# Hybrid attention and short-convolution step: full-height score matmuls, gating units moved last, attention tiles re-placed

## The chip, the cores and the metric

One core of one Trainium2 chip runs the whole kernel. The metric is device time in microseconds (us) of one launch; lower is better. Each engine has its own in-order stream of instructions: TensorE (PE) does matmuls, VectorE (DVE) and ScalarE (ACT) read and write SBUF and PSUM, GpSimd (POOL) does elementwise work, and SyncE (SP) here does little but issue DMAs, in the order in which they were written into its stream.

## The reference, cut to what matters

```python
x = x + 0.5 * rmsnorm(swiglu(rmsnorm(x, f1_pre), f1_wg, f1_wu, f1_wd), f1_post)      # FFN 1
proj = rmsnorm(x, m_pre) @ w_in          # q | k | v | gate B | gate C | conv input
o = attend(q, k, v, lam)                 # 4 heads, two softmax maps per head, width 64 each
u = gate_c * hc
y = sum(conv_w[j] * u_ext[:, j:j + t] for j in range(3))     # u_ext: 2 state rows ahead of u
c_out = gate_b * y
x = x + rmsnorm(concat([o, c_out]) @ w_out, m_post)
x = x + 0.5 * rmsnorm(swiglu(rmsnorm(x, f2_pre), f2_wg, f2_wu, f2_wd), f2_post)      # FFN 2

def diff_attend(q, k, v, q_pos, k_pos, lam):
    s = einsum('bqhcd,bkhcd->bhcqk', q, k) * HEAD_DIM ** -0.5       # c: the two maps
    p = softmax(where(k_pos <= q_pos, s, NEG_INF))
    return einsum('bhqk,bkhe->bqhe', p[:, :, 0] - lam * p[:, :, 1], v)
```

There are 1040 prompt tokens (16 of them meta tokens) and 8 sample sequences of 8 tokens each, which also attend to 1024 past positions held in pages of 128. All data are float32.

## The kernel before

**Precision.** TensorE reads operands in a reduced 32-bit format (fp32r in the rows). To keep float32 results each operand is split by `halves` into a high half (a copy by ACT, L168) and a low half (the original minus the high half, by DVE, L169, or POOL), and a product is made of three matmuls: high x high, high x low, low x high.

**Stages.** FFN 1, then the mixer's projections, then attention, then the output projection, then FFN 2. The 1104 tokens are held in two halves (p = 0 and 1, in the SBUF tiles X0 and X1 with row scales R), features on partitions.

**Projections.** `seven` runs a list of jobs (u, p): unit u of the weights (256 columns of `w_in`, two of the 128-wide column groups paired by `PAIRS`) for token half p. A job is seven products in Strassen's manner, 84 matmuls of 128x276, evicted by ACT and DVE in steps (L347, L350, L353, L356 and the `c..` functions of the unit). The raw weights of one unit lie in one buffer WR (a 1 MB DMA `WR<-in_w_in`); `weights_piece` adds blocks of WR in place on DVE (L273, L275, L277, L279) and writes the seven pieces of the one weight set W (L168, L169). The next unit's load into WR is issued when the last piece of the current one has been made. Units 0 to 5 are q, k and v (`Unit2`). `Product` units multiply gate C and the conv input into `cu` and, with token half 1, call `conv_ready`: three-tap convolution on DVE into `cy`, and DMAs of the new conv state, `out_conv_p` and `out_conv_s`, the latter 1024 rows of 8 bytes. `Gated` units multiply gate B with `cy` into `co` and store that to DRAM (`c_spill`). In the order before, unit 8 is gated and uses the convolutions of 6 and 7; unit 11 is gated and uses those of 9 and 10.

**Attention.** After the projections SP issues the constants `cst`, the queries and keys of head 0 (`load_qk`: one DMA of 128x1040 each), values, lambdas, and the pages of keys and values (`kp`, `vp`; each needs an index read from the page table). `prompt_jobs` makes scores, softmax, transposes (`fl`, L818), and value products (`po`, L833) of one head, block of 128 queries by block; `sample` stages (`sa`, L875, L910) are interleaved with it. In `scores` a head's two maps lie in partitions 0 to 63 and 64 to 127 of the same tile, so a score matmul uses 64 rows of the array (`tile_position`), and the six matmuls of a piece of keys (three passes, two maps) are issued map by turns. PE, DVE, ACT and SP each run their streams in the order in which a scheduler put the instructions.

Of the kernel before, what the change touches and what calls it, by code (L numbers as in the profile page):

```python
# [9 lines left out]
F32R = mybir.dt.float32r  # L10
I32 = mybir.dt.int32
AF = mybir.ActivationFunctionType
ALU = mybir.AluOpType
# [22 lines left out]
         (16, 20), (17, 21), (12, 13), (18, 22), (19, 23), (14, 15)]  # L36
# [7 lines left out]
def hybrid_step(ctx: ExitStack, tc: tile.TileContext, ins, outs, n_pool):  # L44
# [11 lines left out]
    def nm(s):  # L56
        uid[0] += 1
        return f"{s}_{uid[0]}"
# [90 lines left out]
    def dma(dst, src):  # L149
        got = sync.dma_start(dst, src)  # L150
        last_dma[0] = got.ins
        return got
# [13 lines left out]
    def halves(hi, lo, raw, on):  # L166

        act.activation(hi, raw, AF.Copy)  # L168
        on.tensor_tensor(lo, raw, f32(hi), op=ALU.subtract)  # L169
# [337 lines left out]
    def first_jobs(n):  # L507

        return [(0, 0), (1, 0), (1, 1), (0, 1)] + [(u, p) for u in range(2, n) for p in range(2)]
# [82 lines left out]
    cy = [Y[0][:, 1106 + 1104 * n:][:, :1104] for n in range(2)]  # L592
# [4 lines left out]
    def conv_ready(j):  # L597

        taps = [misc[:, j * 3 + t:j * 3 + t + 1] for t in range(3)]
        y, us = cy[j % 2], cs[j % 2]  # L600
# [38 lines left out]
    class Gated(Parts):  # L639


        def __init__(self, j, p):
            self.j, self.p = j, p
            self.o = [co[2 * p], co[2 * p + 1]]

        def put(self, n, g, t):
            y = cy[n][:, self.p * HT + g * G:][:, :G]
            gp.tensor_tensor(self.o[n][:, g * G:g * G + G], t, y, op=ALU.mult)
# [10 lines left out]
        def c21(self, ps):  # L659
            dve.scalar_tensor_tensor(self.o[1][:, :G], ps, -1.0, cy[1][:, self.p * HT:][:, :G], op0=ALU.mult, op1=ALU.mult)  # L660
            for n in range(2):
                dma(c_spill[self.j + n][:, self.p * HT:self.p * HT + HT], self.o[n])

    def mixer_unit(u, p):
        if u < 6:
            return Unit2(u, p)
        return Gated(2 * (u // 9), p) if u in (8, 11) else Product({6: 0, 7: 1, 9: 2, 10: 3}[u], p)

    seven(first_jobs(12), lambda u: ins["w_in"][u], mixer_unit, background)


# [6 lines left out]
    def ring(name, n, w, dt=F32):  # L678
        return [mix.tile([P, w], dt, tag=f"{name}{x}", name=nm(name)) for x in range(n)]


    kpages, vpages = ring("kp", 8, 512), ring("vp", 8, 512)
# [4 lines left out]
    qs_t, = ring("qs", 1, 1024)  # L687
    qs = qs_t.rearrange("p (h b q) -> p h b q", h=H, b=DB)
    ks = ring("ks", 1, 320)[0].rearrange("p (h k) -> p h k", h=H)
# [3 lines left out]
    Q = [ring(f"q{n}", 4, TP, F32R) for n in range(2)]  # L693
    pbuf = ring("p", 6, TP)
    abuf = [a.rearrange("p (j q) -> p j q", j=9) for a in ring("at", 4, 1152)]
    vbuf = [v.rearrange("p (j e) -> p j e", j=9) for v in ring("vs", 2, 1152)]
    tq = ring("t", 10, 256)
    cst, = ring("cst", 1, K_W)
    onesV, = ring("onesV", 1, P)
# [8 lines left out]
    dma(cst, ins["consts"])  # L708

    def load_qk(h):  # L710
        ql, kl, qh, kh = Q[h % 2]
        for lo, hi, src in ((ql, qh, q_spill[h]), (kl, kh, k_spill[h])):
            dma(f32(lo), src[:, :TP])
            halves(hi, lo, f32(lo), dve)
# [5 lines left out]
    load_qk(0)  # L720
    load_v(0)
# [37 lines left out]
    def prompt_jobs(h):  # L759

        pairs = {}
        ql, kl, qh, kh = Q[h % 2]
        vt_ = vbuf[h % 2]

        def scores(qi):
# [7 lines left out]
            for x in range(npc):  # L773
# [3 lines left out]
                for n, (a, b) in enumerate(((qh, kh), (qh, kl), (ql, kh))):  # L777
                    for m in range(2):
                        r = slice(m * DH, (m + 1) * DH)
                        last_pe[0] = nc.tensor.matmul(pw[m], a[r, q0:q0 + P], b[r, k0:k1], start=n == 0, stop=n == 2,  # L780
                                                      tile_position=(m * DH, 0)).ins
# [294 lines left out]
```

## Time and profile before

| | |
|---|---|
| median of 3 runs | 2342.27 us (2340.71 to 2344.84) |
| profiled execution, its own time | 2346.7 us |
| its span | 2344.9 us |
| mean granted TensorE clock | 0.945 of full speed |

The span is the time from the first to the last profiled instruction; what lies around it is 1.8 us. A granted clock of 1.00 in a row is TensorE's upper level (2.4 GHz), 0.50 its lower (1.2 GHz); values in between are means over a stretch with both.

### The profile page before, as it was taken

The page shows a single profiled execution, that of the slowest core. Times are in us where ns is not written, and L with a number is a line of the kernel's source. Part 1 is how long each engine was busy: PE and PEld are TensorE (multiplying, and loading weights), DVE is VectorE, ACT ScalarE, POOL GpSimd, SP SyncE. Part 2 cuts the span into 40 slices and gives each one's busy share as a digit, 9 for nine tenths or more (in the row PEclk, how much of TensorE's full clock was granted, in tenths as well). Part 3 has the DMA queues.
Part 4 walks back from the last instruction along what each step waited for, and adds up shares of the span by engine and source line. Part 5 has one row for each costly group of instructions (what it writes and reads, how often), then busy time and mean ns, then how long its engine had stood idle before and what let it go on. Part 6 is the DMA issues. An engine that isn't in the chain of part 4 may idle for free.

```text
span 2344.9 us, 40781 instructions
## 1 busy us (share of the span) xinstructions
PE 2123.6 (91%) x16266; PEld 2036.9 (87%) x16266; DVE 1373.3 (59%) x2698; ACT 908.3 (39%) x1830; POOL 325.5 (14%) x360
## 2 busy tenths in 40 slices
PE   4899999999999759989689989749999999999995
PEld 4899999999999659989567659749999999999995
DVE  7866666662343985455357653777666666713436
ACT  8533333343211553322245444465333333522112
POOL 0111111121110002221201111001111111301100
PEclk9999999999999879999779979879999999999997
DMA  6122222242332223422557424212122212522213
GB/s 214 56 84 79 75 70 84 79 167 74 110 100 67 96 79 130 141 48 56 174 189 236 162 85 143 78 62 79 63 82 79 84 61 84 174 83 91 98 48 116
DMA packets 106112, 239.29 MB, mean 102 GB/s; under 512 B 20898, under 2 KB 36706, under 8 KB 98274
## 3 DMA queue, kind: packets, MB, share of 16 engines
q1 hardware_dynamic: 105922, 236.70, 30.1%
q8 instruction: 127, 2.08, 0.4%
q14 instruction: 63, 0.52, 0.1%
HBM read 182.35 MB, written 58.82 MB: 103 GB/s over the span
## 4 chain that ended last, share of the span: by engine, by line
PE 78%; DVE 11%; DMA 5%; ACT 3%; issue 2%; SPq 1%; POOL 0%; DVEq 0%; ACTq 0%
PE mm L162 23%; PE mm L163 23%; PE mm L164 23%; DVE X L169 2%; PE qk L780 2%; PE po L833 2%; DMA WR<-in_w_in 2%; DVE W L169 1%; DVE Y L469 1%; PE fl L818 1%; PE sa L910 1%; PE sa L875 1%; DVE ss L210 1%; DVE Y L467 1%; DMA WR<-in_w_gu 1%
## 5 line engine op out<-in xcount | busy, mean ns | idle before, releaser
L162 PE MATMUL mm<-X,W 128*128 128x276 f32 x4224 | 1240.8, 294 | 141.1 <-ACT X L168 100.6
L163 PE MATMUL mm<-X,W 128*128 128x276 f32 x4224 | 1238.7, 293 | 13.4 <-DVE X L169 12.8
L164 PE MATMUL mm<-X,W 128*128 128x276 f32 x4224 | 1234.2, 292 | 5.2 <-DVE W L169 5.2
L162 PEld LDWEIGHTS mm<-X,W 128*128 128x128 f32 x4224 | 803.6, 190 | 148.5 <-ACT X L168 104.2
L163 PEld LDWEIGHTS mm<-X,W 128*128 128x128 f32 x4224 | 804.3, 190 | 17.9 <-DVE X L169 16.3
L164 PEld LDWEIGHTS mm<-X,W 128*128 128x128 f32 x4224 | 805.0, 191 | 7.2 <-DVE W L169 6.7
L168 ACT ACTIVATE W<-WR 128x512 fp32r<-128x512 f32 (+1 forms) x437 | 292.7, 674 | 614.5 <-PE mm L163 526.4
L169 DVE TENSOR_TENSOR W<-WR,W 128x512 fp32r<-128x512 f32 (+1 forms) x437 | 333.9, 766 | 194.0 <-ACT W L168 164.4
L367 POOL TENSOR_TENSOR n<-n,R 128x276 f32<-128x276 f32 x88 | 70.2, 798 | 675.1 <-ACT n L378 675.1
L449 DVE TENSOR_TENSOR Y<-Y,mm 128x276 f32<-128x276 f32 x128 | 56.2, 440 | 168.2 <-PE mm L164 168.0
L350 DVE TENSOR_TENSOR n<-mm,n 128x276 f32<-128x276 f32 x112 | 49.8, 445 | 155.2 <-PE mm L164 155.1
L347 ACT ACTIVATE n<-mm 128x276 f32<-128x276 f32 x224 | 87.7, 392 | 117.0 <-PE mm L164 105.0
L367 POOL TENSOR_TENSOR u<-u,R 128x276 f32<-128x276 f32 x88 | 77.9, 885 | 292.2 <-ACT u L378 292.2
L169 POOL TENSOR_TENSOR X<-X 128x552 fp32r<-128x552 f32 x46 | 75.8, 1658 | 303.0 <-ACT X L168 275.7
L169 DVE TENSOR_TENSOR X<-X 128x552 fp32r<-128x552 f32 x58 | 65.2, 1147 | 79.5 <-ACT X L168 79.5
L163 PE MATMUL mm<-X,X 128*128 128x276 f32 x288 | 83.8, 291 | 2.6 <-DVE X L169 2.6
L168 ACT ACTIVATE X<-X 128x552 fp32r<-128x552 f32 x104 | 66.3, 660 | 48.0 <-DMA X<-hid 41.5
L163 PE MATMUL mm<-X 128*128 128x276 f32 x288 | 84.2, 292 | 0.0
L209 ACT ACTIVATE sq<-Y 128x552 f32<-128x552 f32 x84 | 55.5, 661 | 73.8 <-DVE Y L488 36.3
L780 PE MATMUL qk<-q,q 64*128 64x400 f32 (+10 forms) x360 | 69.5, 392 | 16.1 <-ACT q L168 13.9
L162 PE MATMUL mm<-X,X 128*128 128x276 f32 x288 | 83.5, 290 | 0.0
L164 PE MATMUL mm<-X,X 128*128 128x276 f32 x288 | 83.4, 290 | 0.0
(152 smaller groups left out, 2428.4 us busy)
## 6 DMA issues: line engine op xcount, KB each, us to landing
WR<-in_w_gu SPq DMA_DIRECT2D x46, 1024.0 KB, 5.1
hid<-Y SPq DMA_DIRECT2D x88, 276.0 KB, 2.1
X<-hid SPq DMA_DIRECT2D x88, 276.0 KB, 4.0
WR<-in_w_dnm SPq DMA_DIRECT2D x24, 768.0 KB, 4.2
kp<-in_cache_k SPq DMA_DIRECT2D x64, 256.0 KB, 4.3
vp<-in_cache_v SPq DMA_DIRECT2D x64, 256.0 KB, 4.3
WR<-in_w_in SPq DMA_DIRECT2D x13, 1024.0 KB, 5.4
Y<-in_x SPq DMA_DIRECT2D x16, 276.0 KB, 5.8
```

Of the source, the lines that this page charges most:

```text
L162: nc.tensor.matmul(ps, lh, rh, start=first, stop=False, **kw)
L163: nc.tensor.matmul(ps, lh, rl, start=False, stop=False, **kw)
L164: last_pe[0] = nc.tensor.matmul(ps, ll, rh, start=False, stop=last, **kw).ins
L168: act.activation(hi, raw, AF.Copy)
L169: on.tensor_tensor(lo, raw, f32(hi), op=ALU.subtract)
L209: act.activation(sq, src, AF.Square)
L347: act.activation(t, ps, AF.Copy)
L350: dve.tensor_tensor(self.n1, ps, self.n1, op=ALU.add)
L367: on.tensor_tensor(t, t, lay["R"][p][:, g * G:g * G + G], op=ALU.mult)
L449: dve.tensor_tensor(y, y, ps, op=ALU.add)
L780: last_pe[0] = nc.tensor.matmul(pw[m], a[r, q0:q0 + P], b[r, k0:k1], start=n == 0, stop=n == 2, tile_position=(m * DH, 0)).ins
L833: nc.tensor.matmul(po[:, off:off + rows], vt_[:kr, j, :], at[:kr, j, :rows], start=j == 0, stop=j == qi)
```

## The change

There are three parts. First, `PAIRS` and the job list: units 6 to 9 become the four `Product` units, units 10 and 11 the two `Gated` ones, and the last four jobs are (10,0), (11,0), (11,1), (10,1), so that token half 0 is finished two jobs before the end; unit 10's weights are loaded twice. The four convolution results get four places (`cy`). Second, `load_qk` and `scores`: for each head and map there is a tile q0 or q1 with the high half of 64 query features in partitions 0 to 63 and the low half in 64 to 127, and key tiles kh and kl with the same high or low half in both; a score is two full-height matmuls, q x kh and q x kl, instead of three half-height ones. Each source is loaded twice, into both partition halves. Third, the tiles of the attention stage are allocated in another order, so that the queries and keys of head 0, `cst`, `qs`, `ks`, the small tiles `t` and the pages `kp` take the place of X0, and the queries of head 0 are loaded ahead of `cst`.

```diff
 PAIRS = [(0, 1), (4, 5), (2, 3), (6, 7), (8, 9), (10, 11),
-         (16, 20), (17, 21), (12, 13), (18, 22), (19, 23), (14, 15)]
+         (16, 20), (17, 21), (18, 22), (19, 23), (12, 13), (14, 15)]
...
-    cy = [Y[0][:, 1106 + 1104 * n:][:, :1104] for n in range(2)]
+    cy = [Y[0][:, 1106:2210], Y[0][:, 2210:3314], Y[1][:, 1104:2208], Y[1][:, 0:1104]]
...
-        return Gated(2 * (u // 9), p) if u in (8, 11) else Product({6: 0, 7: 1, 9: 2, 10: 3}[u], p)
-
-    seven(first_jobs(12), lambda u: ins["w_in"][u], mixer_unit, background)
+        return Gated(2 * (u - 10), p) if u >= 10 else Product(u - 6, p)
+
+
+    seven(first_jobs(10) + [(10, 0), (11, 0), (11, 1), (10, 1)], lambda u: ins["w_in"][u], mixer_unit, background)
...
+    scores_of = lambda x: {n: mix.tile([P, TP], F32R, tag=f"{n}{x}", name=nm(n)) for n in ("q0", "q1", "kh0", "kl0", "kh1", "kl1")}
+    cst, = ring("cst", 1, K_W)
+    Q = [scores_of(0)]
...
+    tq = ring("t", 10, 256)
+    kpages = ring("kp", 8, 512)
...
-    dma(cst, ins["consts"])
-
     def load_qk(h):
-        ql, kl, qh, kh = Q[h % 2]
-        for lo, hi, src in ((ql, qh, q_spill[h]), (kl, kh, k_spill[h])):
-            dma(f32(lo), src[:, :TP])
-            halves(hi, lo, f32(lo), dve)
+
+        t = Q[h % 2]
+        for m in range(2):
+            q, kh, kl = t[f"q{m}"], t[f"kh{m}"], t[f"kl{m}"]
+            r = slice(m * DH, m * DH + DH)
+            for i in range(2):
+                at = slice(i * DH, i * DH + DH)
+                dma(f32(q[at]), q_spill[h][r, :TP])
+                dma(f32(kl[at]), k_spill[h][r, :TP])
+            act.activation(kh[DH:], f32(q[DH:]), AF.Copy)
+            dve.tensor_tensor(q[DH:], f32(q[DH:]), f32(kh[DH:]), op=ALU.subtract)
+            act.activation(q[:DH], f32(q[:DH]), AF.Copy)
+            halves(kh, kl, f32(kl), dve)
...
     load_qk(0)
+    dma(cst, ins["consts"])
     load_v(0)
...
-                for n, (a, b) in enumerate(((qh, kh), (qh, kl), (ql, kh))):
-                    for m in range(2):
-                        r = slice(m * DH, (m + 1) * DH)
-                        last_pe[0] = nc.tensor.matmul(pw[m], a[r, q0:q0 + P], b[r, k0:k1], start=n == 0, stop=n == 2,
-                                                      tile_position=(m * DH, 0)).ins
+                for m in range(2):
+                    for n in range(2):
+                        last_pe[0] = nc.tensor.matmul(pw[m], t[f"q{m}"][:, q0:q0 + P], t[f"{('kh', 'kl')[n]}{m}"][:, k0:k1],
+                                                      start=n == 0, stop=n == 1).ins
```

**SP, the second half of the projections.** Here SP's stream before, from the state DMAs of the first convolution to those of the fourth (Y_79 and Y_80 are the tiles Y[0] and Y[1]):

```order
L150 DMA out_conv_p<-Y_79 128x2
L150 DMA out_conv_s<-Y_79 1024x1x2
L150 DMA WR<-in_w_in 128x2048
...
L150 DMA c_spill_161<-Y_80 128x552
L150 DMA WR<-in_w_in 128x2048
L150 DMA out_conv_p<-Y_79 128x2
L150 DMA out_conv_s<-Y_79 1024x1x2
L150 DMA WR<-in_w_in 128x2048
L150 DMA WR<-in_w_out 128x1024 x2
L150 DMA out_conv_p<-Y_79 128x2
L150 DMA out_conv_s<-Y_79 1024x1x2
L150 DMA c_spill_162<-Y_80 128x552
```

And of the change, the same stretch from the third convolution on:

```order
L150 DMA out_conv_p<-Y_79 128x2
L150 DMA out_conv_s<-Y_79 1024x1x2
L150 DMA WR<-in_w_in 128x2048
L150 DMA out_conv_p<-Y_79 128x2
L150 DMA out_conv_s<-Y_79 1024x1x2
L150 DMA WR<-in_w_in 128x2048
L150 DMA c_spill_160<-Y_80 128x552
L150 DMA c_spill_161<-Y_80 128x552
L150 DMA WR<-in_w_in 128x2048
L150 DMA c_spill_162<-Y_80 128x552
```

Before, three of the four state DMAs had a load of `w_in` right behind them and the fourth none; now all four have one, and a further load (unit 10 again) stands behind the first `c_spill` pair.

**SP, from the last projection to the first scores.** Before:

```order
L150 DMA c_spill_162<-Y_80 128x552
L150 DMA WR<-in_w_out 128x1024
L150 DMA c_spill_163<-Y_80 128x552
L150 DMA cst_11242<-in_consts 128x1090
L150 DMA q_673_11212<-q_spill_147 128x1040
L150 DMA q_674_11213<-k_spill_151 128x1040
L150 DMA vs_11230<-v_spill 128x1024
L150 DMA vs_11230<-v_spill 16x128
L150 DMA t_11232<-in_lams 128x256
```

Now:

```order
L150 DMA c_spill_161<-Y_80 128x552
L150 DMA q_650_11208<-q_spill_147 64x1040
L150 DMA kl_653_11211<-k_spill_151 64x1040
L150 DMA q_650_11208<-q_spill_147 64x1040
L150 DMA kl_653_11211<-k_spill_151 64x1040
L150 DMA q_651_11209<-q_spill_147 64x1040
L150 DMA kl_655_11213<-k_spill_151 64x1040
L150 DMA q_651_11209<-q_spill_147 64x1040
L150 DMA kl_655_11213<-k_spill_151 64x1040
L150 DMA cst_11207<-in_consts 128x1090
L150 DMA vs_11235<-v_spill 128x1024
L150 DMA t_11216<-in_lams 128x256
```

The loads of head 0 stand behind the last `c_spill` in both, ahead of `cst` now, and there are eight of them instead of two.

**PE, scores of one query block of head 0.** Before (behind the arrow the key tile, then the query tile; 675 and 676 are the high halves, 673 and 674 the low ones):

```order
L780 MATMUL qk_11879<-q_676_11215,q_675_11214 128x320
L780 MATMUL qk_11879<-q_674_11213,q_675_11214 128x320
L780 MATMUL qk_11879<-q_676_11215,q_673_11212 128x320
L875 MATMUL sa_11657<-kp_11193,qs_11208 32x128 x4
L875 MATMUL sa_11657<-kp_11190,qs_11208 32x128 x4
L780 MATMUL qk_11880<-q_676_11215,q_675_11214 128x320
L875 MATMUL sa_11657<-kp_11194,qs_11208 32x128 x4
...
L780 MATMUL qk_11880<-q_674_11213,q_675_11214 128x320
L780 MATMUL qk_11880<-q_676_11215,q_673_11212 128x320
L780 MATMUL qk_11889<-q_676_11215,q_675_11214 128x336
L780 MATMUL qk_11890<-q_676_11215,q_675_11214 128x336
```

Now:

```order
L794 MATMUL qk_11955<-kh_652_11210,q_650_11208 128x384
L794 MATMUL qk_11955<-kl_653_11211,q_650_11208 128x384
L889 MATMUL sa_11684<-kp_11231,qs_11214 32x128 x4
L889 MATMUL sa_11684<-kp_11228,qs_11214 32x128 x4
L794 MATMUL qk_11956<-kh_654_11212,q_651_11209 128x384
L794 MATMUL qk_11956<-kl_655_11213,q_651_11209 128x384
```

A piece (one pair of qk numbers) had six rows, some of them with the two maps in turn and some with one map's three in a row; it has four now, always one map after the other.

## Rows read from the trace of the kernel before

**Rows 1.** By stretch: us; busy (count) of PE, PEld, DVE, ACT, POOL; PEclk, DMA, GB/s.
```profile
1163.00:1183.00 20.00, 8.46 (x98) 5.71 (x97) 4.37 (x22) 1.33 (x4) 3.44 (x17) 0.50 0.56 174
1202.00:1348.00 146.00, 142.06 (x1305) 98.74 (x1304) 98.77 (x370) 74.14 (x194) 18.20 (x24) 1.00 0.59 192
1348.00:1372.00 24.00, 23.73 (x80) 15.68 (x81) 12.61 (x54) 9.77 (x27) 3.03 (x4) 0.50 0.30 94
```

**Rows 2.** Waits of PE, 880 to 1180: total us, times, longest.
```profile
PE qk L780 <- ACT q L168: 13.9, 1, 13.9
PE mm L162 <- DVE n L353: 12.1, 3, 4.3
PE sa L875 <- POOL qs L746: 7.5, 4, 6.8
```

**Rows 3.** Chain that ended last, 1009 to 1028: start, us, what.
```profile
1010.37 0.13 PE mm L162
...
1013.44 10.47 DMA WR<-in_w_in
...
1025.04 0.60 PE mm L162
1025.64 0.23 PE mm L163
```

**Rows 4.** By stretch, behind the first and the last of three stalls (columns of rows 1).
```profile
1025.04:1032.00 6.96, 6.96 (x35) 6.96 (x36) 4.09 (x7) 0.92 (x2) 1.93 (x2) 0.59 0.00 0
...
1102.32:1108.00 5.68, 5.68 (x32) 5.68 (x33) 3.73 (x7) 0.88 (x2) 1.94 (x2) 0.70 0.00 0
```

**Rows 5.** SP's issues, 1136 to 1164: start, us, what.
```profile
1138.06 0.42 SPq L150 DMA_DIRECT2D c_spill<-Y  x1
1142.73 0.33 SPq L150 DMA_DIRECT2D cst<-in_consts  x1
...
1145.03 0.43 SPq L150 DMA_DIRECT2D t<-in_lams  x1
...
1163.63 0.43 SPq L150 DMA_DIRECT2D t<-q_spill  x1
```

**Rows 6.** Tile q, 1130 to 1400: min/median/max ns, first and last start, forms.
```profile
L168 ACT ACTIVATE q<-q x8: 1055/1070/1072, 1147.8 to 1281.5; 128x1040 fp32r<-128x1040 f32 x8
L169 DVE TENSOR_TENSOR q<-q,q x8: 1236/1242/1244, 1148.9 to 1283.5; 128x1040 fp32r<-128x1040 f32 x8
...
DMA to landing us min/median/max: 4.5/6.3/7.3
```

**Rows 7.** L780 alone, by stretch: us, busy (count) of PE and PEld, PEclk.
```profile
1202.00:1348.00 146.00, 40.17 (x248) 26.13 (x246) 1.00 0.59 192
1348.00:1372.00 24.00, 11.93 (x42) 8.18 (x42) 0.50 0.30 94
```

**Rows 8.** PE's timeline, 1299 to 1312: start, us, what.
```profile
1299.25 0.79 PE L780 MATMUL qk<-q,q 64*128 64x384 f32 x3
1299.97 0.71 PE L833 MATMUL po<-at,vs 128*128 128x128 f32 x4
```

**Rows 9.** The same view, ten us on.
```profile
1310.50 0.89 PE L780 MATMUL qk<-q,q 64*128 64x448 f32 x6
1311.32 0.48 PE L833 MATMUL po<-at,vs 16*128 16x128 f32 x2
```

**Rows 10.** Waits of DVE and ACT, 1185 to 1395.
```profile
DVE p L790 <- PE qk L780: 25.2, 22, 2.2
...
ACT q L168 <- DMA q<-q_spill: 2.5, 2, 1.5
```

**Rows 11.** Chain that ended last, 1392 to 1405 (the last o_spill, the first X load).
```profile
1398.66 0.42 SPq L150
...
1399.27 0.32 SPq L150
```

**Rows 12.** DMA issues, 1392 to 1405: count, KB, us to landing.
```profile
o_spill<-t SPq DMA_DIRECT2D x1, 64.0 KB, 2.7
```

More of the change, by code (lines that the diff above doesn't have):

```diff
@@ L599, in conv_ready @@
         taps = [misc[:, j * 3 + t:j * 3 + t + 1] for t in range(3)]
-        y, us = cy[j % 2], cs[j % 2]
+        y, us = cy[j], cs[j % 2]
         dve.tensor_scalar(y[:, :TP], cu[:, 0:TP], taps[0], None, op0=ALU.mult)
@@ L643, in __init__, with conv @@
             self.j, self.p = j, p
-            self.o = [co[2 * p], co[2 * p + 1]]
+            i = (j // 2 + p) % 2 * 2
+            self.o = [co[i], co[i + 1]]
+        def conv(self, n, g):
+            return cy[self.j + n][:, self.p * HT + g * G:][:, :G]
         def put(self, n, g, t):
-            y = cy[n][:, self.p * HT + g * G:][:, :G]
-            gp.tensor_tensor(self.o[n][:, g * G:g * G + G], t, y, op=ALU.mult)
+            gp.tensor_tensor(self.o[n][:, g * G:g * G + G], t, self.conv(n, g), op=ALU.mult)
         def c11(self, t):
@@ L659, in c21 @@
         def c21(self, ps):
-            dve.scalar_tensor_tensor(self.o[1][:, :G], ps, -1.0, cy[1][:, self.p * HT:][:, :G], op0=ALU.mult, op1=ALU.mult)
+            dve.scalar_tensor_tensor(self.o[1][:, :G], ps, -1.0, self.conv(1, 0), op0=ALU.mult, op1=ALU.mult)
             for n in range(2):
@@ L679, in ring @@
         return [mix.tile([P, w], dt, tag=f"{name}{x}", name=nm(name)) for x in range(n)]
-    kpages, vpages = ring("kp", 8, 512), ring("vp", 8, 512)
+    scores_of = lambda x: {n: mix.tile([P, TP], F32R, tag=f"{n}{x}", name=nm(n)) for n in ("q0", "q1", "kh0", "kl0", "kh1", "kl1")}
+    cst, = ring("cst", 1, K_W)
+    Q = [scores_of(0)]
+    qs_t, = ring("qs", 1, 1024)
+    qs = qs_t.rearrange("p (h b q) -> p h b q", h=H, b=DB)
+    ks = ring("ks", 1, 320)[0].rearrange("p (h k) -> p h k", h=H)
+    tq = ring("t", 10, 256)
+    kpages = ring("kp", 8, 512)
+    onesV, = ring("onesV", 1, P)
+    vbuf = [v.rearrange("p (j e) -> p j e", j=9) for v in ring("vs", 2, 1152)]
+    pbuf = ring("p", 6, TP)
+    abuf = [a.rearrange("p (j q) -> p j q", j=9) for a in ring("at", 4, 1152)]
     s_p, = ring("s_p", 1, 1104)
@@ L686, in hybrid_step @@
     s_comb, = ring("s_comb", 1, 64)
-    qs_t, = ring("qs", 1, 1024)
-    qs = qs_t.rearrange("p (h b q) -> p h b q", h=H, b=DB)
-    ks = ring("ks", 1, 320)[0].rearrange("p (h k) -> p h k", h=H)
     o_t, = ring("o_s", 1, 256)
@@ L692, in hybrid_step @@
     v_new = ring("v_new", 1, 512)[0][:80]
[L693 to L699, printed above, removed]
+    vpages = ring("vp", 8, 512)
+    Q.append(scores_of(1))
     gp.memset(onesV, 1.0 / DV)
@@ L761, in prompt_jobs @@
         pairs = {}
-        ql, kl, qh, kh = Q[h % 2]
+        t = Q[h % 2]
         vt_ = vbuf[h % 2]
```

## The prediction

> **What bounds the kernel now.** I read the kernel stretch by stretch, because its limits differ. The sum over stretches first [rows 1]: from 1202 to 1348 us, the bulk of attention, PE is busy 142.06 of 146.00 us at full clock, while DVE has 98.77 and ACT 74.14. Here PE decides, and a shorter PE stream is a shorter stretch. From 1163 to 1183 PE has work for only 8.46 of 20 us: data are late there. From 1348 to 1372 PE is full again, 23.73 of 24.00 us, but at half clock. Then PE's list of waits [rows 2] for the places where it stands still in and behind the projections: 13.9 us once, before the first scores; 12.1 us in three waits on an eviction (L353); 7.5 us on `qs`, of which one wait is 6.8 us.
>
> What lies under the three waits is seen in the chain that ended last [rows 3]: the load of WR, issued at 1013.44 right behind the 1024-row state DMA, takes 10.47 us; the evictions that PE needs stand on DVE behind the addition that reads WR, so PE restarts at 1025.04, and its matmuls of 276 columns then come every 0.23 us instead of every 0.13. So a stall costs its wait plus a stretch at half clock. Behind the first stall the granted clock is 0.59 over 6.96 us, behind the third 0.70 over 5.68 us [rows 4]: 6.96 x 0.41 = 2.9 and 5.68 x 0.30 = 1.7 us lost. With 2.3 us for the middle one, the three cost 12.1 + 6.9 = 19.0 us, 6.3 us each.
>
> **The change, part by part.**
>
> *Gating units last.* In SP's stream three state DMAs of four had a WR load right behind them, now all four have one. The fourth conv's DMAs were free before, since `w_out` was already under way. So there is one stall more, in job (10,0): **+6.3 us**. Its lower bound is 0 (if the WR load there is issued late enough to pass the small DMA rows by), its upper bound 8.5 us: in (10,0) the weights change at once, so that an addition and a split (0.7 us each by their places in the chain, an estimate) can come on top of the worst of the three, 4.3 + 2.9 = 7.2 us. The repeated load of unit 10 adds a set of weight pieces to ACT and DVE, spread over a job of about 84 x 0.13 = 11 us, and both engines have room beside PE in the projections; I take 0, at most 2.6 us if the pieces arrive as they do in a stall, with the clock kept.
>
> *From the last projection to attention.* Before, `cst` was issued at 1142.73, 4.67 us behind the last `c_spill` (1138.06), because it had to wait until that had landed; q and k followed, and the first score waited 13.9 us in all [rows 2, 5]. Now q0 stands in the place of X0, which PE has left two jobs earlier. But SP's order still has it behind the last `c_spill`, which waits for the last eviction, so the head start of two jobs isn't used; q0 can leave some 0.5 us behind that `c_spill`, 4.6 us earlier than q did. Against that there are eight loads at about 0.45 us of SP each where there were two, six copies on ACT of up to 1.07 us where there were two, and four subtractions on DVE of up to 1.24 us [rows 6]. Fourth load issued near 1140, landed 4.5 to 7.3 us later [rows 6], a copy and a subtraction (2.3 us): first scores of map 0 at 1147 to 1150, of map 1 after three to four more copies and a subtraction, 1151 to 1155; before, 1150 to 1151.5. That doesn't set the end of this stretch either: SP's own sequence does, up to `t` from `q_spill`, issued at 1163.63 [rows 5], on which `qs` and PE's 6.8 us wait depend. The lambdas, the last load before the page indices, were issued at 1145.03; with six more loads in the queue, one of them waiting until `c_spill` has landed, I expect 1145.3 to 1147.5. **+1.2 us**, from -2 to +4.
>
> *Scores.* An L780 piece was six matmuls, and what six cost depends on their neighbours. Three of one map in a row, 384 columns, take 1299.97 - 1299.25 = 0.72 us [rows 8]; a piece has two such, 1.44 us. All six in turn, 448 columns, take 0.82 us [rows 9]: there the two maps run side by side. A full-height matmul takes 0.13 us for 276 columns [rows 3], so four take 0.72 us at 384 columns and 0.84 us at 448. A separated piece halves, an interleaved one stays as it is. In PE's timeline from 1202 to 1348 the groups of L780 are 50, of which 17 are threes and 11 sixes; at 0.13/276 us per column and four for six, what took 40.17 us busy [rows 7] (39.0 us from start to start) takes 24.9 us: -14.1 us, 36%. The same share of the 11.93 us from 1348 to 1372 [rows 7], where PE is full as well, is -4.3 us, and I put -1 us for the end of attention. The stretch before 1202 I count at nothing, since late data rule it [rows 1]. Together -19.4 us. Not all of it arrives: DVE, which waits 25.2 us for score matmuls now [rows 10], will run nearer to its limit, and the transposes that wait for softmax come up earlier. I take **-16.5 us**, with -22.5 (everything, the stretch before 1202 too) and -8 (the softmax chain takes over half of it) as bounds.
>
> *Halves in both partitions.* For heads 1 to 3 the loads are eight DMAs instead of two, four ACT operations more (4 x 1.07 = 4.3 us) and two DVE operations more (2.5 us) per head, all inside the stretch where PE decides. ACT has 72 us of room there, DVE 47 [rows 1], so the work itself is hidden; but it stands in order: ACT waits for q's DMA already (2.5 us in two waits [rows 10]), with softmax exponentials and evictions behind it, and SP's pages stand behind the six extra issues (2.7 us). Without cover all three heads would cost 3 x 4.3 = 13 us. **+3 us**, from 0 to +10.
>
> *FFN 2's entry.* The first X load was issued at 1399.27, 0.6 us behind the last `o_spill` (1398.66) [rows 11], which left from `t`. X0 now covers `t`, so the load waits until these stores have landed: 2.7 us for such a store [rows 12], less the 0.6 to 0.8: **+1.9 us**, from 1 to 3.
>
> Sum: 6.3 + 1.2 - 16.5 + 3 + 1.9 = -4.1 us on the profiled 2346.7, or 0.17%; 2342.27 - 4.1 = **2338.2 us** against the median, which lies 4.4 below the profiled execution. What a measurement of this kernel can tell from no change is about 0.2%, 4.7 us: below 2337.6 is faster, above 2347.0 slower.
>
> **The rivals.**
>
> *Slower: the extra halves hold up ACT.* Place: the three changes of heads, where the copies of the next head's tiles stand on ACT ahead of exponentials and evictions. If a copy reaches the head of ACT's queue before its DMA has landed (before: 2.5 us in two waits), the softmax, hence the transposes, hence PE wait. For it: three times as many copies, each behind a DMA of its own, SP's issues in one line. Against it: the loads are issued well ahead of a head's first scores. It decides when it costs over 12 us, 3 to 4 us per head; at its upper bound of 10 us for the halves, with the stall at 8.5 and scores at -14, the sum is 8.5 + 2 - 14 + 10 + 1.9 = +8.4, **2351 us**.
>
> *Softmax takes over.* PE's stream shrinks, but DVE and ACT turn over the same softmax; then scores give -8 and the sum is +4.4: 2347 us. For it DVE's 68% share [rows 1]; against it DVE's waits for PE.
>
> *The clock's lapse goes away.* From 1348 to 1372 the clock is 0.50 with PE busy 99% [rows 1]: no gap of PE's stream explains it. With other work in that place it may not come. The 24 us, 20 after the shorter scores, would be done in 10 to 12 (DVE's 12.6 us is the floor): -8 to -10 us, 2338.2 - 9 = **2329 us**. The same may come in at another place: it is as uncertain as the lapse.
>
> *Side by side is worth more.* Two half-height matmuls can run at once: all six in 0.82 us at 448 columns [rows 9], where four full-height ones take 0.84. If most pieces did so, the scores term would be about 0 and the time 2342.3 + 12.4 = 2355 us. The threes [rows 8] and the 40.17 us of the window [rows 7] say that most don't; all sixes would have made it some 25. The Trainium skill's "TensorEngine Tiling (Array Packing)", section "The Solution" with "Theoretical Speedup", has a gain of up to two times for contractions of at most 64 rows by tiling the rows, which speaks against full height; this trace agrees for the sixes alone.
>
> *The early tiles do hide the gap.* If SP got q and k out two jobs ahead, up to 13 us would go: 2325 us. SP's order speaks against it.
>
> **How the numbers follow.** The forecast's own case 0.44 (2330 to 2346), halves or stall worse 0.22, softmax takes over 0.12, no lapse 0.14, side by side 0.03, gap hidden 0.05. Of the forecast's case nearly half lies below 2337.6. Faster: 0.20 + 0.14 + 0.05 and a little of the rest, 0.41; same: 0.23 + 0.08 + 0.02, 0.33; slower: 0.26. The range 2327 to 2351 leaves out the hidden gap, side by side and the ends of both neighbours.
>
> **What the changed profile would show.** A fourth wait of PE on an L353-like eviction in (10,0) with a WR load of 10 us under it (right), or three waits only (stall term wrong). Score matmuls of 128 rows, 165 where 248 stood, with some 25 us where 40 were. q0's DMA right behind the last `c_spill`, first scores at 11 to 14 us behind the last projection, `qs` as late as before. ACT waits on q and kl DMAs of 5 to 8 us in place of 2.5; over 12, and the slower rival holds. The first X load 2 to 3 us behind the last `o_spill`. A clock of 0.50 between some 1330 and 1360; none there, and the third rival holds. The prediction is wrong if PE's waits inside attention grow beyond 10 us, or if the clock lapses in a new place.

## The result and the profile after

The changed kernel took 2358.39 us (median of 20 runs, 2354.64 to 2363.88), the kernel before 2343.40 us (20 runs, 2338.31 to 2358.56): a ratio of 1.0052, 95% interval 1.0038 to 1.0065. The forecast was 2338.2 us with a range of 2327 to 2351; the change is slower by 15 us on the medians and lies above the range. The profiled spans are 2344.9 us before and 2359.1 after. One run of `e4_only_jobs` below, at 4234.74 us, was a slow one and is left out of its median.

I laid both traces side by side at three points of PE's timeline: the last projection matmul, the first `sa` (the first matmul of the sample sequences) and the first matmul behind attention. That one belongs to the output projection; the prediction calls the place FFN 2's entry, but FFN 2 comes later.

| stretch | before, us | after, us | difference |
|---|---|---|---|
| up to the last projection matmul | 1136.0 | 1148.3 | +12.3 |
| from there to the first `sa` | 33.9 | 36.7 | +2.8 |
| first `sa` to the output projection's first matmul | 233.4 | 232.1 | -1.3 |
| the rest | 941.6 | 942.0 | +0.4 |

**Projections.** PE's waits from 880 to 1180 us after (total us, times, longest), against [rows 2]:

```profile
PE qk L794 <- ACT kh L168: 17.6, 2, 15.3
PE mm L162 <- DVE n L353: 14.7, 3, 5.3
PE mm L162 <- ACT W L168: 6.6, 2, 6.0
```

There is a fourth stall, in (10,0), and PE waits there 6.0 us for a weight piece; the three old ones grew from 12.1 to 14.7 us. The chain that ended last through the new stall (start, us, what), against [rows 3]:

```profile
1098.33 11.01 DMA WR<-in_w_in
...
1109.97 0.44 DVE n L353
1110.41 0.61 DVE W L169
...
1111.66 0.23 PE mm L162
```

The same chain as in the three old stalls, with one piece more (DVE W) because the weights change at once, and a lower clock behind it. By stretch (us; busy and count of PE, PEld, DVE, ACT, POOL; PEclk, DMA share, GB/s), behind the first stall and the new one, against [rows 4]; then the place where the clock had lapsed before, against [rows 1]:

```profile
1025.50:1032.00 6.50, 6.46 (x31) 6.46 (x32) 3.63 (x7) 0.72 (x2) 1.93 (x2) 0.57 0.00 0
...
1110.00:1118.00 8.00, 7.77 (x38) 7.45 (x38) 7.35 (x13) 3.77 (x8) 2.10 (x2) 0.60 0.12 46
...
1348.00:1372.00 24.00, 23.40 (x238) 18.50 (x237) 17.41 (x68) 11.90 (x35) 3.37 (x5) 1.00 0.52 168
```

**To attention.** SP's issues after, against [rows 5]:

```profile
1151.04 0.38 SPq L150 DMA_DIRECT2D c_spill<-Y  x1
1151.51 0.50 SPq L150 DMA_DIRECT2D q<-q_spill  x1
...
1155.90 0.60 SPq L150 DMA_DIRECT2D kl<-k_spill  x1
...
1178.93 0.61 SPq L150 DMA_DIRECT2D t<-q_spill  x1
```

As predicted, q0 leaves 0.47 us behind the last `c_spill`. But the eight issues take 0.63 us each, not 0.45, and SP's sequence up to `t` from `q_spill` ends 30.6 us behind the last projection matmul, where it was 27.6. From DMA issues, then from tile q, against [rows 6]:

```profile
q<-q_spill SPq DMA_DIRECT2D x4, 260.0 KB, 7.9
```

```profile
L725 ACT ACTIVATE kh<-q x8: 1066/1067/1070, 1159.4 to 1320.9; 64x1040 fp32r<-64x1040 f32 x8
L726 DVE TENSOR_TENSOR q<-q,kh x8: 1237/1239/1526, 1160.5 to 1322.0; 64x1040 fp32r<-64x1040 f32 x8
```

A load takes 7.9 us to land, and a copy or subtraction of 64 partitions costs what one of 128 did; ACT has six copies for a head, where there were two. The loads are slower too. By stretch while they are under way, first before (128 partitions each), then after (64 each):

```profile
1146.00:1149.00 3.00, 0.00 (x0) 0.00 (x0) 0.06 (x1) 1.07 (x1) 0.00 (x0) 0.50 1.02 413
1158.00:1164.00 6.00, 0.05 (x1) 0.05 (x1) 1.31 (x2) 3.09 (x3) 0.00 (x0) 0.50 1.04 212
```

The 16 DMA engines are busy throughout in both (1.02 and 1.04), but move 212 GB/s in place of 413. Twice the bytes at half the rate: the loads of a head occupy the engines for about 10 us instead of 2.6 (an estimate from these rates and the sizes, 8 x 260 KB and 2 x 520 KB).

**Attention.** The whole stretch before, from the first `sa` on, in the columns above:

```profile
1169.90:1396.00 226.10, 215.76 (x1735) 150.30 (x1735) 139.70 (x512) 105.20 (x268) 27.81 (x47) 0.88 0.50 164
```

and after, with L794 alone in two of its parts at full clock (PE and PEld only), against [rows 7]:

```profile
1185.00:1409.00 224.00, 197.13 (x1624) 140.13 (x1624) 147.66 (x518) 116.09 (x280) 30.23 (x46) 0.94 0.61 180
...
1256.50:1310.50 54.00, 14.18 (x60) 8.94 (x60) 1.00 0.71 212
1315.00:1409.00 94.00, 24.96 (x100) 15.05 (x100) 1.00 0.45 142
```

PE's idle time grew from 226.10 - 215.76 = 10.3 us to 224.00 - 197.13 = 26.9, +16.5. What the clock withheld fell from 226.1 x 0.12 = 27.1 us to 224.0 x 0.06 = 13.4, -13.7. The work itself, busy time by clock, fell from 189.9 to 185.3 us: -4.6 where -19.4 was worked out. The last two rows show it on the scores alone: 160 full-height matmuls are busy for 14.18 + 24.96 = 39.1 us, and 248 half-height ones were for 40.17. From start to start, as the forecast counted, the 160 take 34.8 us where its rate gives 24.8. PE's timeline after (start, us, what), against [rows 8, 9], shows part of the reason:

```profile
1324.15 0.31 PE L794 MATMUL qk<-kl,q 128*128 128x320 f32 x1
1324.29 0.31 PE L794 MATMUL qk<-kh,q 128*128 128x320 f32 x1
1324.44 0.31 PE L794 MATMUL qk<-kl,q 128*128 128x320 f32 x1
...
1329.59 0.45 PE L794 MATMUL qk<-kh,q 128*128 128x400 f32 x1
1329.88 0.34 PE L794 MATMUL qk<-kl,q 128*128 128x400 f32 x1
1330.06 0.60 PE L832 MATMUL fl<-cst,p 128*128 128x128 f32 x4
```

Among themselves score matmuls follow at 0.14 to 0.15 us for 320 columns, at the predicted rate (0.13/276 us a column). The first behind another group holds the next up for 0.29 us at 400 columns, the second for 0.18. Of the 49 pieces from 1206 us on, 27 are two pairs apart and pay some 0.1 us twice. The 160 matmuls above stand in 46 groups, so this price explains 4.6 of their 10 us (an estimate); what takes the rest I have not found.

Where the idle time is, by PE's waits from 1180 to 1430:

```profile
PE mm L162 <- ACT X L168: 8.0, 1, 8.0
PE sa L889 <- POOL qs L761: 5.6, 4, 5.1
PE sa L889 <- DMA kp<-in_cache_k: 5.3, 4, 3.8
PE po L847 <- DVE at L834: 5.0, 2, 4.9
```

Waits of ACT and DVE, 1200 to 1408, against [rows 10]:

```profile
ACT q L727 <- DMA q<-q_spill: 9.6, 3, 7.5
...
ACT kh L725 <- DMA q<-q_spill: 4.2, 4, 1.4
DVE q L726 <- ACT kh L725: 7.6, 3, 5.0
```

DVE's and PE's timelines show how such a wait reaches PE:

```profile
1221.27 1.24 DVE L726 TENSOR_TENSOR q<-q,kh 64x1040 fp32r<-64x1040 f32 x1 [2.26 <-ACT kh L725]
1222.54 0.28 DVE L834 COPY at<-fl 16x128 f32<-16x128 f32 x1
...
1222.87 0.79 PE L847 MATMUL po<-at,vs 16*128 16x128 f32 x2 [4.86 <-DVE at L834]
```

The subtraction of the next head waits on DVE for ACT's copy, which waits for its DMA; the eviction of the transposes stands behind the subtraction, and PE stands still for 4.86 us. It costs more than the wait, since the clock is low behind it (columns as above):

```profile
1222.00:1230.00 8.00, 7.13 (x31) 6.03 (x31) 7.13 (x19) 3.90 (x8) 0.00 (x0) 0.57 0.11 36
```

Behind other waits it is 0.72 from 1246 to 1258 and from 1310 to 1316. With 0.63 from 1185 to 1198, at the start, these stretches hold all that the clock withheld: 3.4 + 3.4 + 1.7 + 4.8 = 13.3 us.

**The output projection.** The chain after, against [rows 11, 12]: the last `o_spill` lands, then SP issues the first load of X0 (the second row).

```profile
1411.68 1.58 DMA o_spill<-t
...
1413.46 0.32 SPq L150
```

PE's wait at this entry was 7.19 us before and is 7.95 after: +0.8.

### The profile page after: what moved, and what is told of

Same layout as the page of the kernel before. It is cut to its first block, busy times and chain, and to the rows that moved or that the text cites. A ratio compares the mean times of both kernels' runs of the same rounds, so it can differ in the third digit from the quotient of the medians.

```text
span 2359.1 us, 40620 instructions
## 1 busy us (share of the span) xinstructions
PE 2108.3 (89%) x16146; PEld 2029.9 (86%) x16146; DVE 1390.2 (59%) x2717; ACT 928.0 (39%) x1853; POOL 329.5 (14%) x360
## 4 chain that ended last, share of the span: by engine, by line
PE 74%; DVE 11%; DMA 8%; ACT 3%; issue 2%; SPq 1%; POOL 0%; DVEq 0%; ACTq 0%; POOLq 0%
PE mm L162 23%; PE mm L163 23%; PE mm L164 23%; DMA WR<-in_w_in 2%; DVE X L169 2%; DVE W L169 1%; PE po L847 1%; DMA q<-q_spill 1%; DVE Y L469 1%; PE qk L794 1%; DMA kp<-in_cache_k 1%; SPq L150 1%; DVE ss L210 1%; DVE Y L467 1%; PE fl L832 1%
## 5 line engine op out<-in xcount | busy, mean ns | idle before, releaser
L163 PEld LDWEIGHTS mm<-X,W 128*128 128x128 f32 x4224 | 806.5, 191 | 16.3 <-DVE X L169 14.5
L169 DVE TENSOR_TENSOR X<-X 128x552 fp32r<-128x552 f32 x58 | 64.0, 1125 | 82.0 <-ACT X L168 81.8
L273 DVE TENSOR_TENSOR WR<-WR 128x512 f32<-128x512 f32 x60 | 46.2, 769 | 66.5 <-DMA WR<-in_w_in 46.4
```

The lines of the kernel that those rows point to most:

```text
L163: nc.tensor.matmul(ps, lh, rl, start=False, stop=False, **kw)
L273: dve.tensor_tensor(a3, a11, a21, op=ALU.add)
```

## The experiments

Ratios are against the kernel before on the same chip, with 95% intervals. Theory A was that the state stores ahead of weight loads make the stalls; theory B that feeding the doubled halves eats what the scores give. The rivals stand in the expectations; in those of e3 and e7 to e10, A and B mean something narrower, the loads and the copies.

Runs of one kernel spread with their mean granted clock: 124 runs of the kernel before, on these chips, took 2334 to 2359 us, with a median of 2337.9 at a clock of 0.950 and of 2349.4 at 0.944, or some 1.9 us for 0.001. So where two kernels ran at different clocks, their medians differ by that as well, and I say so.

| kernel | median, us | ratio |
|---|---|---|
| the change | 2358.4 | 1.0052 (1.0038 to 1.0065) |
| e1_old_jobs | 2354.7 | 1.0048 (1.0026 to 1.0070) |
| e2_state_late | 2329.1 | 0.9941 (0.9919 to 0.9964) |
| e4_only_jobs | 2354.3 | 1.0052 (1.0027 to 1.0077) |
| e5_before_late | 2326.1 | 0.9921 (0.9890 to 0.9952) |
| e11_jobs_late | 2328.8 | 0.9922 (0.9892 to 0.9952) |
| e6_only_scores | 2351.5 | 1.0028 (1.0012 to 1.0044) |
| e13_scores_one_head | 2331.2 | 0.9937 (0.9914 to 0.9959) |
| e7_after_one_head | 2347.6 | 1.0014 (0.9998 to 1.0030) |
| e8_before_one_head | 2344.2 | 0.9992 (0.9966 to 1.0018) |
| e9_before_loads | 2354.1 | 1.0040 (1.0020 to 1.0059) |
| e10_before_copies | 2361.5 | 1.0078 (1.0049 to 1.0106) |
| e3_wide_loads | 2480.9 | 1.0575 (1.0552 to 1.0599) |
| e18_pool_feed | 2339.2 | 0.9972 (0.9954 to 0.9990) |
| e12_late_actq | 2334.4 | 0.9964 (0.9945 to 0.9983) |
| e14_late_early_q | 2339.8 | 0.9983 (0.9967 to 0.9999) |
| e15_old_scores_early_q | 2334.2 | 0.9962 (0.9935 to 0.9990) |
| e16_held_w_out | 2330.2 | 0.9927 (0.9900 to 0.9954) |
| e17_held_new_scores | 2330.4 | 0.9932 (0.9908 to 0.9955) |

### The order of the units

`e4_only_jobs` is the kernel before with the new `PAIRS`, `cy` and job list alone; `e1_old_jobs` is the change with the old ones.

> The kernel before with only the new order of units and jobs. Theory (order costs 12 us by itself): 2343.4 + 12 = 2355 us, four waits of PE on the eviction or the weight pieces behind a load of 10 to 11 us. Rival (6 us): 2349 us.

> The changed kernel with the old order of units and jobs (gated units 8 and 11, first_jobs(12), two places for the convolution results, unit 10 loaded once); stacked query halves and tile placement stay. Theory (the new job order costs 12 us: a fourth wait on a slow weight load, in a job that changes weights): last projection matmul 12 us earlier, time 2358.4 - 12 = 2346 us. Rival (the order costs the 6 us of one more stall as predicted, the rest is lost in attention): 2352 us.

The order alone costs 2354.3 - 2344.3 = 10.0 us on the medians. PE's waits in e4, 990 to 1145:

```profile
PE mm L162 <- DVE n L353: 12.5, 3, 4.4
PE mm L162 <- ACT W L168: 5.2, 1, 5.2
```

The fourth stall is the order's. This profile is of a run of 2342.8 us at a clock of 0.949, among the fastest of runs that go up to 2366 us at 0.939, so part of the 10 us is the clock. In it the last projection matmul starts at 1142.67, 6.65 us later than before, near the predicted 6.3. In the change it starts 12.3 us later: its four loads ahead of the stalls take 10.70 to 11.44 us, those of e4 10.08 to 10.55, and why is open. Taken out of the change the order gives only 3.7 us: in e1 attention ran at a mean clock of 0.88 and not 0.94, which gave most of it back. That is no accident of one run: the seven runs of e1 have mean clocks of 0.941 to 0.945, the twenty of the change 0.944 to 0.952.

`e2_state_late` and `e5_before_late` issue the state DMAs behind the next weight load, in the changed kernel and in the one before:

```diff
-        dma(outs["conv_s"][j], us[:, :, 8:10])
+        late.append((outs["conv_s"][j], us[:, :, 8:10]))    # conv_p likewise
...
                         weights_of(src(order[0]))
+                while late:
+                    with tc.issue_after(last_dma[0]):
+                        dma(*late.pop(0))
```

> The changed kernel with the two state DMAs of each convolution issued right behind the next weight load instead of right ahead of it. Theory (the 1024 rows of 8 bytes ahead of the load make it 10 to 11 us instead of 5): loads land in 5 us, the four waits (21 us) and the half clock behind them (about 5 us) go: 2358.4 - 24 = 2334 us. Rival (the load is slow in that place whatever stands ahead of it, or the state rows slow it from behind as well): less than 6 us gained, 2353 us or more.

> The kernel before with the same edit. Theory: its three waits (12 us) and the half clock behind them (7 us) go: 2343.4 - 19 = 2324 us. Rival: 2340 us or more.

Of e2, DMAs issued from 1005 to 1035 (count, KB, us to landing):

```profile
WR<-in_w_in SPq DMA_DIRECT2D x2, 1024.0 KB, 5.0
...
out_conv_s<-Y SPq DMA_DIRECT2D x1, 8.0 KB, 11.0
```

The load takes 5.0 us in place of 10 to 11, and the stalls of PE go: from 990 to 1125 e2 keeps this wait and one of 0.8 us, e5 none.

```profile
PE mm L164 <- DVE W L169: 3.1, 3, 1.8
```

That is worth 29 us in the change and 18 in the kernel before. Theory A is shown, for the two state DMAs together; no run moves one of them alone. `e11_jobs_late` has the new order and the late state DMAs in the kernel before:

> The kernel before with the new order of units and jobs and with the state DMAs behind the weight loads. If the order costs only through the state rows ahead of a weight load: as the kernel before with late state DMAs, 2326 us. If it has a cost of its own (unit 10 twice, weights changed in a job of token half 0): 2331 us or more.

2328.8 us beside e5's 2326.1: with the stores out of the way the order costs nothing that these runs can tell.

### The scores and what feeds them

`e6_only_scores` is the kernel before with the new `load_qk` and `scores` in the old tile places. In `e13_scores_one_head` (from e6), `e7_after_one_head` (from the change) and `e8_before_one_head` (from the kernel before) heads 1 to 3 use head 0's tiles; their loads and copies are left out:

```diff
-            load_qk(step // 9 + 1)
...
-        t = Q[h % 2]
+        t = Q[0]
```

> The kernel before with only the full-height scores and their loads; units, jobs and the places of the tiles as before. If the score part itself costs attention 4 to 10 us: 2343.4 + 8 = 2351 us, waits in attention some 15 us above the kernel before. If the places of the tiles were to blame in e1_old_jobs: 2345 us or less.

> The kernel before with full-height scores alone, and without the loads and copies of queries and keys for heads 1 to 3, whose scores use head 0's tiles (work left out, outputs not the reference's). Beside the yardstick (the same omission with the old scores, 2344.2 us) it shows the score matmuls without what feeds them. If the term of the prediction was right (-16.5 us) and only the feeding cost more: 2328 us. If the matmuls gain about half of it, because each pair that stands alone pays some 0.1 us: 2336 us. If nothing: 2344 us.

> The changed kernel without the loads and copies of queries and keys for heads 1 to 3, whose scores use head 0's tiles instead (work left out, so their outputs are not the reference's). If the extra loads and copies make the new waits in attention (A or B), PE's waits from the first sample matmul to the end of attention fall from 32 to some 16 us: 2345 us, and a gain clearly above that of the same edit in the kernel before. Rival C (PE simply finishes scores sooner and waits for softmax): waits stay near 28 us, 2354 us.

> The same edit in the kernel before, as the yardstick (work left out in the same way). With A or B right: a gain of 2 to 5 us, 2340 us; with C right: about as much as in the changed kernel.

Attention by windows, first e8, then e13, then e6:

```profile
1169.70:1394.10 224.40, 215.17 (x1735) 148.76 (x1735) 134.40 (x506) 99.96 (x262) 28.62 (x46) 0.89 0.47 151
```

```profile
1173.60:1381.00 207.40, 194.30 (x1624) 135.62 (x1624) 132.46 (x506) 98.47 (x262) 27.68 (x46) 0.96 0.51 164
```

```profile
1172.00:1402.20 230.20, 204.09 (x1624) 148.24 (x1624) 147.74 (x518) 116.39 (x280) 27.53 (x46) 0.88 0.59 175
```

Before, feeding is free (e8). Without feeding, the new scores are worth 2344.2 - 2331.2 = 13 us; feeding them costs 2351.5 - 2331.2 = 20 us in e6 and 2358.4 - 2347.6 = 11 in the change. Between e8 and e13 the work shrinks by 215.17 x 0.89 - 194.30 x 0.96 = 5 us, idle time grows by 4, and the clock gives back 224.4 x 0.11 - 207.4 x 0.04 = 16. The runs say the same: five of e8's twelve have a mean clock of 0.949 or more, and their median is 2333.5 us, 2 us above e13, whose nine runs all have. In e6 the clock is 0.88 again and PE is idle for 26 us, with most of the half clock right behind idle time. Its runs have mean clocks of 0.942 to 0.946, e13's 0.949 to 0.954, so by those 1.9 us for 0.001 more than half of the 20 us is clock (an estimate); e7 and the change ran at like clocks.

`e9_before_loads` is the kernel before with eight DMAs of 64x1040 per head in place of its two, half of them into spare tiles; `e10_before_copies` adds only four ACT copies of 64x1040 and two DVE subtractions per head.

```diff
+            for r, o in ((slice(0, DH), slice(DH, P)), (slice(DH, P), slice(0, DH))):   # e9
+                dma(f32(lo[r]), src[r, :TP])
+                dma(f32(d[o]), src[r, :TP])
...
+            for r in (slice(0, DH), slice(DH, P)):                                      # e10
+                act.activation(d[r], f32(lo[r]), AF.Copy)
+            dve.tensor_tensor(d, f32(lo), f32(d), op=ALU.subtract)
```

> The kernel before with queries and keys of each head loaded by eight DMAs of 64x1040, as in the changed kernel, half of them into spare tiles that nothing reads; scores and copies as before. Theory A (the half-height loads themselves cost: their rate and SP's queue): +6 to +8 us, 2352 us, first scores and first sample matmul later by 3 us together. Theory B (the copies cost): +2 us at most, 2346 us.

> The kernel before with four more ACT copies of 64x1040 and two more DVE subtractions of 128x1040 per head into spare tiles that nothing reads, each waiting for the head's loads; loads and scores as before. Theory B: +6 to +8 us, 2352 us, waits of PE in attention up by 10. Theory A: +2 us at most, 2346 us.

Loads alone cost 9 us, copies alone 16, and the two do not add up to what e6 shows. In e9 PE waits 17.4 us for the first score, where it was 13.9, and 7.7 for `kp` pages, where it was 4.2: 7 of the 9 us. In e10 no wait of PE grew by more than 2 us; its attention took 235.8 us at a clock of 0.87, and why stays open. Its six runs have mean clocks of 0.939 to 0.946, so part of the 16 us is clock.

`e3_wide_loads` loads both halves with one DMA whose source is repeated, four a head instead of eight:

```diff
+            for to, src in ((q, q_spill[h]), (kl, k_spill[h])):
+                dma(f32(to), src[r, :TP].unsqueeze(0).to_broadcast([2, DH, TP]))
```

> The changed kernel with four loads of 128x1040 per head (the same 64 source rows read twice by one DMA) instead of eight of 64x1040: the same bytes, half the issues. Theory A (loads of 64 partitions run slowly and fill SP's queue, so queries and pages are late): first scores 4 us earlier, waits in attention down by 8 us, 2358.4 - 8 = 2350 us. Theory B (the copies standing in order on ACT and DVE hold attention up): less than 2 us gained, 2357 us.

Neither theory had this: PE waited 49.9 us for two copies behind these loads.

The row of windows for ten microseconds in which little else was under way:

```profile
1165.00:1175.00 10.00, 0.38 (x1) 0.29 (x1) 1.10 (x2) 1.16 (x2) 0.00 (x0) 0.50 0.13 52
```

The Trainium skill's "DMA: Bandwidth & Descriptors", section "Rules for kernel authors", says that an outermost dimension smaller than 16, such as a leading broadcast of c copies, confines a DMA to c of the 16 engines; the share of 0.13, two of 16, agrees.

`e18_pool_feed` is e2 with the copies and subtractions of heads 1 to 3 on POOL, out of ACT's and DVE's streams:

> The changed kernel with late state DMAs (2329 us), and for heads 1 to 3 all copies and subtractions of queries and keys on POOL instead of ACT and DVE. If the cost of feeding the scores is the copies' place in ACT's and DVE's order: 2329 - 8 = 2321 us. If it is the loads, or POOL's scaling of the softmax is held up instead: 2329 us or more.

10 us worse than e2. A subtraction takes POOL about 2.4 us. PE's waits for DVE's `at`, 6.0 us in e2, fall to 0.9, so that part of the price is gone; but those for `vp` pages grow from 0.5 to 5.3 us, and those for `kp` stay (5.6 and 5.4). What POOL's added work costs by itself these runs do not show, so e18 does not part the loads from the order on ACT and DVE.

### The gap ahead of attention

All of these have the late state DMAs. `e12_late_actq` issues head 0's loads on ACT's queue; `e14_late_early_q` puts the `w_out` loads and the last two `c_spill`s there, so that SP's stream frees head 0's loads early; `e15_old_scores_early_q` is e14 with the old scores and loads.

```diff
+                put = act.dma_start if h == 0 else dma      # e12
-                dma(f32(q[at]), q_spill[h][r, :TP])
+                put(f32(q[at]), q_spill[h][r, :TP])
...
-            dma(raw, wsrc)                                  # e14, e15
+            (act.dma_start if g_post == G_MPOST else dma)(raw, wsrc)
```

> The changed kernel with late state DMAs, and the eight loads of head 0 issued by ACT instead of SP, so that they stand ahead of the last store of gated values and SP is free for pages. If SP's order keeps the early tiles from paying: first scores and first sample matmul some 5 us earlier, 2329 - 5 = 2324 us. If the loads' own rate sets it: 2328 us.

> The changed kernel with late state DMAs, and with the loads of w_out and the last two stores of gated values issued by ACT, so that on SP the loads of head 0 stand right behind the stores of job (11,1), a job ahead of the end. If SP's order was what kept the early tiles from paying: first scores 8 us sooner after the last projection (7 instead of 15.6 us), first sample matmul as well, 2329 - 10 = 2319 us. If not: 2327 us or more.

> The same with the old scores and their two loads per head (new unit order, new places of the tiles). With the early loads paying and the score part costing: 2326 - 12 = 2314 us. Without: 2326 us.

None closed it. In e12 PE waits 19.95 us, since the loads stand on ACT behind work that waits for `w_out`. In e14 the first score waits 14.5 us, by the profile for `cst`; ACT's copy of its keys ends at the same moment. In e15 head 0's loads had landed before the last projection matmul, and ACT's timeline shows what was ahead of the copies:

```profile
1132.40 1.06 ACT L168 ACTIVATE W<-WR 128x1024 fp32r<-128x1024 f32 x1 [5.48 <-DMA WR<-in_w_out]
...
1135.12 2.03 ACT L168 ACTIVATE q<-q 128x1040 fp32r<-128x1040 f32 x2 [1.67 <-DVE W L169]
```

ACT makes pieces of `w_out` first, each behind its DMA. So `e16_held_w_out` (old scores) and `e17_held_new_scores` hold these loads until head 0's have been issued, with the last two `c_spill`s on ACT's queue:

```diff
     load_qk(0)
+    held[0] = last_dma[0]
...
+            with tc.issue_after(held[0]) if g_post == G_MPOST else nullcontext():
+                dma(raw, wsrc)
```

> The kernel before with the new order of units and jobs, the new places of the tiles, late state DMAs, old scores; the last two stores of gated values issued by ACT, and the loads of w_out held back until behind head 0's loads. In the run with early loads, head 0's keys had landed before the last projection ended, but ACT made three pieces of w_out first, each waiting for its load. If that is what keeps the gap: first scores 5 us behind the last projection instead of 15, 2328.8 - 10 = 2319 us. If not, or if the pieces of w_out then disturb attention as much: 2328 us.

> The changed kernel with late state DMAs and the same hold on w_out and the two stores on ACT. If the gap closes: 2329 - 8 = 2321 us, first scores 7 us behind the last projection. If the eight loads and six copies of head 0 fill the gap anyway: 2328 us.

The gap closes: the first score comes 4.1 us behind the last projection matmul in e16 and 6.0 in e17, where it was 14 to 16; and yet neither is faster than e5 or e2. Attention of e16 takes 236.5 us where that of e11 takes 226.2; the third row is a part of e16's:

```profile
1143.60:1380.10 236.50, 221.22 (x1735) 150.58 (x1735) 144.46 (x515) 108.18 (x271) 28.49 (x46) 0.89 0.51 166
1154.70:1380.90 226.20, 214.16 (x1735) 146.88 (x1735) 139.43 (x512) 105.09 (x268) 27.72 (x46) 0.89 0.49 164
1223.90:1247.50 23.60, 23.60 (x147) 15.86 (x148) 9.61 (x35) 7.37 (x20) 3.35 (x5) 0.50 0.62 205
```

The ten microseconds won at the entry are spent inside. The mean clock is not the difference: it is 0.89 in both, and both have one long stretch at half clock with PE full, e11's from 1332 to 1358 at 0.54. The pieces of `w_out`, made inside attention now, are the likeliest reason, argued from DVE's and ACT's busy time (5 and 3 us more in e16) and not shown.

## Why the prediction was wrong

**Halves in both partitions, +3 us.** This is the step whose size failed most: 11 us in the change and 20 in e6, both beyond the upper bound of 10. The prediction took the work as hidden by ACT's and DVE's free time and bounded the order at 3 to 4 us a head. The mechanism of the slower rival held: ACT's waits for q's loads went from 2.5 to 13.8 us (9.6 + 4.2), past its mark of 12, and reached PE through DVE's stream. What I had put at nothing are the loads themselves, worth 9 us in e9: I let a load of half the height land in the time of a full one, and it moved 212 GB/s in place of 413. The Trainium skill's "DMA: Bandwidth & Descriptors", section "Rules for kernel authors", says that two transfers to disjoint partition halves serialize because they share the same 16 engines, and advises one of 128 partitions. The trace agrees that all engines are taken while these loads run (a share of 1.04 from 1158 to 1164).

**Scores, -16.5 us.** Measured without feeding, -13 us: the size nearly held by luck, and its working failed. The step "a full-height matmul takes 0.13 us for 276 columns, so four take 0.72 us at 384" took a rate from the projections, where such matmuls follow one another. Here the first of a group pays 0.1 us more, 27 of 49 pieces are in two groups, and 160 matmuls take 34.8 us from start to start where the rate gives 24.8. PE's work fell by 5 us in place of 19.4; the rest of the gain came with the clock, which is the rival "the clock's lapse goes away".

**The stall, +6.3 us.** The mechanism held. The order alone moved the end of the projections by 6.65 us in e4, as predicted, but by 12.3 in the change. There the new stall lasts 6.0 us and leaves 8.00 us at clock 0.60, 3.2 us lost: 9.2, above the bound of 8.5, which rested on the worst of the old stalls. Another 2.6 us are the old three, 14.7 in place of 12.1. Why the loads under them took longer than in e4 is open.

**The entry to attention, +1.2 us.** +2.8, inside -2 to +4. Right: the early places of the tiles do not help by themselves. Of the rival "the early tiles hide the gap", e15 and e16 show why it could not: first SP's order, then ACT's pieces of `w_out`, and behind both an attention that takes the time back.

**"FFN 2's entry", +1.9 us.** It is the output projection's entry, and cost +0.8: the last `o_spill` landed in 1.58 us, not 2.7.

**The signs of being wrong.** Both came: PE's idle time inside attention grew by 16.5 us, and the clock lapsed in new places, behind these waits.

**The other rivals.** The old lapse of the clock did go: 1.00 from 1348 to 1372, where it was 0.50, and over attention the clock gave 13.7 us back; PE's idle time took them. Whether full-height matmuls keep the clock up is not shown. A stretch of some 24 us or more at 0.50 to 0.54 with PE full stands in four of the nine profiles with the old scores (before, e5, e11, e16) and in none of the eleven with the new ones; e6 and e1 have a mean of 0.88 in attention all the same, with most of the half clock behind idle time. Softmax did not take over: in e13, with the same softmax, attention takes 207.4 us. Side by side was worth more than I thought: a piece of two pairs at 400 columns passes in 2 x (0.29 + 0.18) = 0.94 us, so the threes [rows 8] gained and the sixes [rows 9] lost.

In sum, 12.3 + 2.8 - 13 + 11 + 0.8 = +13.9 us, beside +14.2 between the two spans. That it comes so close is partly luck: three terms are stretches of one profile each, -13 and +11 differences of medians.

## What to carry to other kernels

Look at what stands in a DMA queue ahead of a large load: moving two small stores behind it was worth 18 us here, without the change (2326.1 us, the lowest median of this study, with e2 and e11 3 us above), three times what any term of the change promised to cost. Split a load over partition halves only if its time is hidden: here that halved its rate. Price a matmul by rows in which it stands among the same neighbours as it will, since the first of a group costs more than the next. Free time of an in-order engine hides work only if the data of that work are there when it comes to the head of the stream: ask for each added operation what stands behind it. Before a gain is put down to shorter work, compare runs at like granted clocks.

## What the runs showed of the hardware

- Two small stores, the larger of 1024 rows of 8 bytes, ahead of a 1 MB load in SP's stream make the load take 10 to 11 us; with them behind it, it takes 5.0 us, and the larger one then takes 11.0 in place of 8.8.
- Loads into 64 partitions moved 212 GB/s with all 16 DMA engines busy (1.04), loads into 128 partitions 413 GB/s (1.02).
- DMAs from a repeated source moved 52 GB/s, at a share of 0.13 of the 16 engines. The first two issues of e3 took SP 0.60 and 0.77 us, the next two 8.54 and 10.91, and the plain load of `cst` behind them 9.99.
- Half clock came behind idle time (0.57 from 1222 to 1230, behind 4.86 us without work), and in some kernels with PE full: 0.50 from 1223.90 to 1247.50 in e16, with PE busy for all of the 23.60 us.
- The first full-height matmul behind another group costs about 0.1 us more, also behind `po`, whose tile in the rows is 128*128 like its own:

```profile
1262.10 0.90 PE L847 MATMUL po<-at,vs 128*128 128x128 f32 x4
1262.93 0.42 PE L794 MATMUL qk<-kh,q 128*128 128x320 f32 x1
1263.18 0.31 PE L794 MATMUL qk<-kl,q 128*128 128x320 f32 x1
1263.33 0.31 PE L794 MATMUL qk<-kh,q 128*128 128x320 f32 x1
```

Here 0.25 us pass from the first score matmul to the next and then 0.15, with no other array shape right ahead.
